# MLP up-projection with the tokens stationary, and the squared features turned by DMA transposes of 16-bit planes

## The chip, the cores and the metric

The kernel is one program on one core of a Trainium2 chip. The metric is the time of one execution on the device in microseconds (us); the value of a kernel is the median of its runs. The engines are named as in the profile: PE (TensorE, the matrix engine; PEld is its loading of stationary tiles), ACT (ScalarE), DVE (VectorE), POOL (GpSimd) and SP (SyncE), whose queue issues all DMAs of this kernel.

## The reference

Two layers over 256 tokens of width 2048, all in float32. A layer is a token mixer, a cross-attention into 256 memory tokens, and a dense MLP; each is wrapped in RMS norms and added to the residual stream. The change touches the MLP alone:

```
def squared_relu_mlp(h, w_up, w_down):          # h 256 x 2048, w_up 2048 x 8192, w_down 8192 x 2048
    return jnp.square(jax.nn.relu(h @ w_up)) @ w_down

y = squared_relu_mlp(rms_norm(h, g_mlp_pre[l]), w_up[l], w_down[l])
h = h + rms_norm(y, g_mlp_post[l])
```

## The kernel before, in words

**Split products.** Every large product is made of three matmuls. A float32 operand is split into a high part in the matmul's own type (float32r, `h` for weights, first plane of `xt` for activations) and the rest (`l`, second plane), and high x high, high x low and low x high are summed in PSUM.

**Weights.** They are streamed as units of two 128-row tiles by 512 columns (512 KB), in the order of use. For each unit `load` issues a DMA into one of 5 `r` buffers; `convert` lets ACT write the high part `h` (times the norm's gain `gT`, one instruction for each tile, where there is a gain) and then DVE the low part `l`, into one of 8 pairs of buffers. A load waits until DVE has read the unit that was 5 earlier from the same buffer; a conversion waits until PE has used the unit that was 8 earlier.

**The MLP.** The 8192 hidden features are taken in 4 groups (`q`) of 2048. In a group, 4 up panels (`p`) of 512 features are computed over 16 k-tiles (8 units), and then 4 down panels of 512 output columns over the group's 16 tiles of hidden features (8 units). The down panels go through `gemm_a`: a 128x128 tile of hidden features is stationary and 512 weight columns move, 96 matmuls to a panel, 3 for each k-tile and token block (`tb`, 128 tokens each). Since the stationary tile must have the features on its partitions, the hidden features are needed with features on partitions and tokens along the free axis.

**Up panels.** All but the first of a layer go through `gemm_w`: 128 weight columns are stationary and the tokens move, so the result has its features on the partitions already. For each k-tile and each of 4 column blocks there is one matmul of 512 columns (the weights' `h` by both planes of `xt`) and one of 256 (`l` by the high plane). Four PSUM banks come out, one for each block, each with the two halves side by side; `relu2` adds the halves, clamps, squares and splits into `h` and `lo`. The first up panel of a layer goes through `gemm_a` (tokens stationary, one token block after the other), and `relu2_t` turns its result round with four PE transposes to a token block.

**Order.** The program is written out ahead of time by one pass that keeps its own estimate of each engine's clock. `spawn` puts a side task on a heap, `run_side` continues those whose time has come, and `yield self.when(tile)` sets the task aside until the estimate says that the tile is there. Each engine then works through its own list in order, and SP its DMAs in order too. All engine calls go through a recording wrapper, so every instruction of before has line 84 in the profile, whatever function it comes from; the names of tiles tell them apart. In names, `p` is a PSUM bank, `t` a scratch tile (hidden features among them), `xt` the MLP's input, turned; PE rows give the moving operand first and the stationary one second.

Of the kernel before, what the change touches and what calls it, by code (L numbers as in the profile page):

```python
# [12 lines left out]
F32 = mybir.dt.float32  # L13
F32R = mybir.dt.float32r
I32 = mybir.dt.int32
AF = mybir.ActivationFunctionType
OP = mybir.AluOpType
AX = mybir.AxisListType
# [98 lines left out]
class Gen:  # L117
# [169 lines left out]
    def convert(self, u):  # L287
# [7 lines left out]
        if u.gains is None:  # L295
            a = slice(0, n)
            nc.scalar.activation(u.h[:, :, a], u.raw[:, :, a], AF.Copy)
            (nc.gpsimd if u.pool else nc.vector).tensor_sub(u.l[:, :, a], u.raw[:, :, a], u.h[:, :, a].bitcast(F32))
        else:
            for k in range(u.nk):  # L300
                g = self.gain_col(u.gains[k])
                nc.scalar.activation(u.h[:, k, :n], u.raw[:, k, :n], AF.Copy, scale=g)
                if u.pool:
# [127 lines left out]
    def rsqrt(self, out, v, eng=None, times=None):  # L431
# [38 lines left out]
    def square_sum(self, src, out):  # L470
        self.nc.scalar.activation(self.junk[:, :src.shape[-1]], src, AF.Square, accum_out=out)


    def setup(self):
# [28 lines left out]
        nc.sync.dma_start(self.cst[:, 128:], io["cst"][:, 128:])  # L503
        posi = c.tile([128, 4], I32, name="posi")
        nc.sync.dma_start(posi[:, 0:2], io["positions"].rearrange("o (t p) -> p (o t)", p=128))
# [9 lines left out]
        def more():  # L515
# [3 lines left out]
            nc.tensor.transpose(b[:, 128:224], graw3[0:96, :], self.ident[0:96, 0:96])  # L519
            nc.scalar.activation(self.gT[:, 32:128], b[:, 128:224], AF.Copy)  # L520
            nc.tensor.transpose(b[:, :80], graw2[0:80, :], self.ident[0:80, 0:80])
            nc.scalar.activation(self.gT[:, 128:208], b[:, :80], AF.Copy)
            yield self.T_TAB
# [913 lines left out]
    def mlp(self, l, P, last):  # L1437
        nc = self.nc
        ep, rs = self.ep, self.rs
        lhs, mov, both = self.xlhs(ep), self.xmov(), self.xboth()  # L1440
        y = [[None] * 4, [None] * 4]
        ssq = [self.st(), self.st()]

        def relu2(banks, pair):
            r = self.tt((2, 256))
            for j in range(2):
                nc.scalar.activation(r[:, j, :], banks[j][:, 256:512], AF.Copy)
            for j in range(2):
                nc.vector.tensor_add(r[:, j, :], banks[j][:, 0:256], r[:, j, :])
            nc.vector.scalar_tensor_tensor(r, r, 0.0, r, op0=OP.max, op1=OP.mult)  # L1450
            h, lo = pair
            nc.scalar.activation(h, r, AF.Copy)
            nc.vector.tensor_sub(lo, r, h.bitcast(F32))

        def relu2_t(tb, bank, pairs):
            r = self.tt()
            nc.scalar.activation(r, bank, AF.Relu)
            nc.vector.tensor_mul(r, r, r)
            yield self.when(r)
            b = self.ps()  # L1460
            for j in range(4):
                nc.tensor.transpose(b[:, j * 128:j * 128 + 128], r[:, j * 128:j * 128 + 128], self.ident)
            a = slice(tb * 128, tb * 128 + 128)
            v = b.rearrange("p (k t) -> p k t", k=4)
            for j in range(2):
                nc.scalar.activation(pairs[j][0][:, :, a], v[:, 2 * j:2 * j + 2, :], AF.Copy)
            for j in range(2):
                h, lo = pairs[j]
                nc.vector.tensor_sub(lo[:, :, a], v[:, 2 * j:2 * j + 2, :], h[:, :, a].bitcast(F32))
            self.ready.add(("up0", l, tb))  # L1470
        for q in range(4):
            hid = []
            for p in range(4):
                pairs = [(self.tt((2, 256), F32R), self.tt((2, 256), F32R)) for _ in range(2)]
                hid += pairs
                if q + p == 0:
                    for tb in range(2):
                        b = self.gemm_a(P["up", 0], lhs, (tb,))
                        self.spawn(relu2_t(tb, b[tb], pairs))
                        self.run_side()  # L1480
                else:
                    banks = self.gemm_w(P["up", 4 * q + p], 4, mov, both)
                    for j in range(2):
                        relu2(banks[2 * j:2 * j + 2], pairs[j])
            if q == 3:
                post = self.load_post("g_mlp_post", l)
                XT = None if last else self.new_xt()
                r2 = self.st()
                nc.vector.tensor_mul(r2[:, 0:2], rs[:, 0:2], rs[:, 0:2])
                nc.vector.tensor_mul(r2[:, 2:4], r2[:, 0:2], r2[:, 0:2])  # L1490
                nc.vector.tensor_scalar(r2[:, 2:4], r2[:, 2:4], 1.0 / D, None, op0=OP.mult)

            def hlhs(kt, tb):
                if q == 0:
                    self.require(("up0", l, tb))
                h, lo = hid[kt // 2]
                a = slice(tb * 128, tb * 128 + 128)
                return h[:, kt % 2, a], lo[:, kt % 2, a]

            def evac(tb, p, bank):  # L1500
                if q == 0:
                    y[tb][p] = self.tt()
                    nc.scalar.activation(y[tb][p], bank, AF.Copy)
                else:
                    nc.vector.tensor_add(y[tb][p], y[tb][p], bank)
                if q == 3:
                    self.square_sum(y[tb][p], ssq[tb][:, p:p + 1])
                    yg = self.tt()
                    nc.vector.tensor_mul(yg, y[tb][p], post[p])
                    y[tb][p] = yg  # L1510
            for p in range(4):
                if q == 3 and p == 3:
                    for tb in range(2):
                        self.part_mean(ssq[tb], r2[:, 2 + tb:3 + tb])
                    for tb in range(2):
                        b = self.gemm_a(P["dn", q, p], hlhs, (tb,))
                        evac(tb, p, b[tb])
                        self.spawn(self.chain(tb, y[tb], ssq[tb], XT, self.rs, self.ep, r2, late=8.0))
                        self.run_side()
                else:  # L1520
                    b = self.gemm_a(P["dn", q, p], hlhs)
                    for tb in range(2):
                        evac(tb, p, b[tb])

# [47 lines left out]
```

## Time and profile before

| | us |
|---|---|
| median of 3 runs (lowest to highest) | 2470.06 (2468.72 to 2470.64) |
| the profiled execution, own time | 2468.55 |
| its span, first to last instruction | 2466.7 |
| PE busy in the span | 2434.4 (99%) |
| DVE busy | 1555.5 (63%) |
| ACT busy | 1333.0 (54%) |

The profiled execution lasts 1.85 us longer than its span, and lies 1.51 us below the median. PE is busy nearly without a break. Matmuls are pipelined, so the length of one record is not what one costs; the distance between the starts of two that follow each other is. Where an instruction names itself `p<-xt,h` it is a matmul of `gemm_w`; `p<-h,xt` is the first up panel (and the mixer's projections) and `p<-h,t` a down panel, both of `gemm_a`.

### The profile page before, as it was taken

Reading aid. Unit: us, or ns where it says so; the run is one execution under the profiler, and the core shown is the slowest. Engines: PE = TensorE matmul, PEld = TensorE weight load, DVE = VectorE, ACT = ScalarE, POOL = GpSimd, SP = SyncE. Lnnn points to the kernel's source line nnn. Section 1 sums busy time; section 2 is a strip of 40 time slices with the busy share of each in tenths; the row PEclk is TensorE's granted clock in tenths of the full one; section 3 lists DMA queues with packets and bytes.
Section 4 is the critical chain, followed back from the end, with each engine's and each line's share of the span. In section 5 each row is a group of like instructions: output and inputs, shape, how many; then the busy total and the mean of one; then the engine's idle time right before and its main releaser. Section 6 shows DMA issues by size and latency. Waiting matters only on the chain.

```text
span 2466.7 us, 34746 instructions
## 1 busy us (share of the span) xinstructions
PE 2434.4 (99%) x12803; PEld 2104.2 (85%) x12803; DVE 1555.5 (63%) x2738; ACT 1333.0 (54%) x2283; POOL 154.3 (6%) x266
## 2 busy tenths in 40 slices
PE   8999999999999999999999999999999999999998
PEld 7999988888888888888878999987788888888886
DVE  6767757566546656556576577647864565665665
ACT  7665656666545445445447566546754554544542
POOL 2000002122000000000021000004300000000001
PEclk9999999999999999999999999999999999999999
DMA  7555565546666566565646464654556656666662
GB/s 255 159 169 150 152 210 177 195 156 198 200 194 187 188 194 188 188 195 172 222 145 188 127 194 122 211 166 154 179 182 199 183 193 193 184 192 195 187 206 102
DMA packets 263207, 447.36 MB, mean 181 GB/s; under 512 B 21550, under 2 KB 77566, under 8 KB 263038
## 3 DMA queue, kind: packets, MB, share of 16 engines
q1 hardware_dynamic: 263038, 445.16, 58.1%
q8 instruction: 100, 1.64, 0.3%
q14 instruction: 69, 0.57, 0.1%
HBM read 443.00 MB, written 2.10 MB: 180 GB/s over the span
## 4 chain that ended last, share of the span: by engine, by line
PE 90%; DVE 4%; ACT 2%; POOL 1%; issue 1%; DMA 1%; SPq 0%; POOLq 0%; ACTq 0%; DVEq 0%
PE p L84 90%; DVE l L84 2%; ACT h L84 1%; DVE t L84 1%; DVE s L84 1%; POOL s L84 1%; DVE xt L84 0%; DMA r<-in_w_in_dram 0%; DMA t<-in_x_dram 0%; POOL r L84 0%; SPq L84 0%; ACT junk L84 0%; ACT t L84 0%; POOL t L84 0%; POOL l L84 0%
## 5 line engine op out<-in xcount | busy, mean ns | idle before, releaser
L84 PE MATMUL p<-h,t 128*128 128x512 f32 (+3 forms) x3072 | 934.5, 382 | 0.0
L84 DVE SCALAR_TENSOR_TENSOR l<-r,gT,h 128x512 fp32r<-128x512 f32 (+3 forms) x998 | 672.6, 726 | 274.9 <-ACT h L84 272.4
L84 ACT ACTIVATE h<-r,gT 128x512 fp32r<-128x512 f32 (+3 forms) x1008 | 635.0, 688 | 287.5 <-PE p L84 156.5
L84 PE MATMUL p<-xt,h 128*128 128x512 f32 x1920 | 678.9, 399 | 0.0
L84 PEld LDWEIGHTS p<-h,t 128*128 128x128 f32 (+1 forms) x3072 | 565.0, 185 | 109.3
L84 DVE TENSOR_TENSOR l<-r,h 128x1024 fp32r<-128x1024 f32 x346 | 423.0, 1232 | 368.4 <-ACT h L84 367.1
L84 PE MATMUL p<-l,t 128*128 128x512 f32 (+3 forms) x1536 | 584.8, 381 | 0.0
L84 ACT ACTIVATE h<-r 128x1024 fp32r<-128x1024 f32 x352 | 367.9, 1057 | 378.9 <-PE p L84 360.4
L84 PE MATMUL p<-xt,l 128*128 128x256 f32 x1920 | 539.2, 281 | 0.0
L84 PE MATMUL p<-h,xt 128*128 128x384 f32 (+3 forms) x1664 | 497.3, 367 | 2.2 <-ACT h L84 2.1
L84 PEld LDWEIGHTS p<-xt,h 128*128 128x128 f32 x1920 | 360.8, 188 | 89.8
L84 PEld LDWEIGHTS p<-xt,l 128*128 128x128 f32 x1920 | 362.7, 189 | 0.3
L84 PEld LDWEIGHTS p<-h,xt 128*128 128x128 f32 x1664 | 308.8, 188 | 32.5 <-ACT h L84 2.5
L84 PEld LDWEIGHTS p<-l,t 128*128 128x128 f32 (+1 forms) x1536 | 283.6, 185 | 53.7
L84 PE MATMUL p<-l,xt 128*128 128x384 f32 (+3 forms) x832 | 299.9, 360 | 2.9 <-POOL l L84 1.4
L84 ACT ACTIVATE t<-p 128x256 f32<-128x256 f32 (+6 forms) x336 | 140.9, 445 | 124.6 <-PE p L84 123.0
L84 PEld LDWEIGHTS p<-l,xt 128*128 128x128 f32 x832 | 156.9, 189 | 17.1 <-DVE l L84 2.8
L84 POOL TENSOR_SCALAR t<-t,s 128x512 f32<-128x512 f32 x12 | 25.4, 2113 | 1752.6 <-DVE s L84 1743.7
L84 DVE TENSOR_TENSOR t<-p,t 128x256 f32<-128x256 f32 (+3 forms) x220 | 98.1, 474 | 43.5 <-ACT junk L84 18.9
L84 PE MATMUL p<-t,t 128*128 128x128 f32 (+5 forms) x624 | 110.0, 310 | 0.0
L84 PEld LDWEIGHTS p<-t,t 128*128 128x128 f32 (+3 forms) x624 | 93.7, 192 | 14.4 <-issue 1.3
L84 DVE TENSOR_TENSOR t<-t,t 128x512 fp32r<-128x512 f32 (+6 forms) x119 | 74.4, 625 | 46.7 <-ACT t L84 44.8
(77 smaller groups left out, 1136.4 us busy)
## 6 DMA issues: line engine op xcount, KB each, us to landing
r<-in_w_up_dram SPq DMA_DIRECT2D x256, 512.0 KB, 4.2
r<-in_w_down_dram SPq DMA_DIRECT2D x256, 512.0 KB, 4.3
r<-in_w_in_dram SPq DMA_DIRECT2D x96, 384.0 KB, 3.7
r<-in_w_out_dram SPq DMA_DIRECT2D x64, 512.0 KB, 4.0
r<-in_w_in_dram SPq DMA_DIRECT2D x47, 512.0 KB, 4.6
r<-in_w_xkv_dram SPq DMA_DIRECT2D x32, 512.0 KB, 4.0
r<-in_w_xq_dram SPq DMA_DIRECT2D x16, 512.0 KB, 4.2
r<-in_w_xo_dram SPq DMA_DIRECT2D x16, 512.0 KB, 4.3
```

The costliest lines, as they stand in the source:

```text
L84: r = f(*a, **k)
```

## The change

All up panels now go through `gemm_a`, tokens stationary, and their results have the tokens on the partitions. A new `relu2` turns them round for each token block: ACT applies the ReLU out of PSUM, DVE squares, DVE copies the 512 float32 values as 1024 16-bit halves into two planes (all even halves, then all odd ones), SP issues one DMA that transposes the 128x1024 tile of 16-bit numbers in 128x128 blocks, ACT puts the planes together again into float32 and copies out the high part, and DVE forms the low part. The PE transposes of the first panel go. The loads of the post-norm's gain stand after the first down panel of the last group, where they stood ahead of it.

```diff
-        lhs, mov, both = self.xlhs(ep), self.xmov(), self.xboth()
+        lhs = self.xlhs(ep)
...
-        def relu2(banks, pair):
-            r = self.tt((2, 256))
-            for j in range(2):
-                nc.scalar.activation(r[:, j, :], banks[j][:, 256:512], AF.Copy)
-            for j in range(2):
-                nc.vector.tensor_add(r[:, j, :], banks[j][:, 0:256], r[:, j, :])
-            nc.vector.scalar_tensor_tensor(r, r, 0.0, r, op0=OP.max, op1=OP.mult)
-            h, lo = pair
-            nc.scalar.activation(h, r, AF.Copy)
-            nc.vector.tensor_sub(lo, r, h.bitcast(F32))
-
-        def relu2_t(tb, bank, pairs):
+        def relu2(flag, bank, h, lo):
             r = self.tt()
             nc.scalar.activation(r, bank, AF.Relu)
             nc.vector.tensor_mul(r, r, r)
-            yield self.when(r)
-            b = self.ps()
-            for j in range(4):
-                nc.tensor.transpose(b[:, j * 128:j * 128 + 128], r[:, j * 128:j * 128 + 128], self.ident)
...
+            halves = r.bitcast(U16).rearrange("p (n e) -> p e n", e=2)
+            planes = self.tt((2, 512), U16)
+            nc.vector.tensor_copy(planes, halves)
+            yield self.when(planes)
+            turned = self.tt((8, 128), U16)
+            nc.sync.dma_start(turned, planes.rearrange("p e n -> p (e n)"), transpose=True)
+            yield self.when(turned)
+            nc.scalar.activation(halves, turned.rearrange("p (e a) b -> p e (a b)", e=2), AF.Copy)
+            v = r.rearrange("p (a b) -> p a b", b=128)
+            nc.scalar.activation(h, v, AF.Copy)
+            nc.vector.tensor_sub(lo, v, h.bitcast(F32))
+            self.ready.add(flag)
...
-                    banks = self.gemm_w(P["up", 4 * q + p], 4, mov, both)
-                    for j in range(2):
-                        relu2(banks[2 * j:2 * j + 2], pairs[j])
+                    b = self.gemm_a(P["up", 4 * q + p], lhs)
+                    for tb in range(2):
+                        self.spawn(relu2(("up", l, q, p, tb), b[tb], *hid[p][tb]))
+                    self.run_side()
...
             def hlhs(kt, tb):
-                if q == 0:
-                    self.require(("up0", l, tb))
-                h, lo = hid[kt // 2]
+                self.require(("up", l, q, kt // 4, tb))
+                h, lo = hid[kt // 4][tb]
...
                     b = self.gemm_a(P["dn", q, p], hlhs)
+                    if q == 3 and p == 0:
+                        post = self.load_post("g_mlp_post", l)
```

**PE in an up panel.** Before, one k-tile of a panel (`h1598` and `l1598` hold its weights, the four banks are p1594 to p1597) stands so on PE:

```order
L84 MATMUL p1594_9376<-xt1076_3_5538,h1598_9388 128x512
L84 MATMUL p1594_9376<-xt1076_3_5538,l1598_9389 128x256
L84 MATMUL p1595_9377<-xt1076_3_5538,h1598_9388 128x512
L84 MATMUL p1595_9377<-xt1076_3_5538,l1598_9389 128x256
L84 MATMUL p1596_9378<-xt1076_3_5538,h1598_9388 128x512
L84 MATMUL p1596_9378<-xt1076_3_5538,l1598_9389 128x256
L84 MATMUL p1597_9379<-xt1076_3_5538,h1598_9388 128x512
L84 MATMUL p1597_9379<-xt1076_3_5538,l1598_9389 128x256
```

With the change, one k-tile stands so (two banks, p1492 for the first token block and p1493 for the second):

```order
L85 MATMUL p1492_7942<-h1472_7851,xt1076_1_5536 128x512
L85 MATMUL p1492_7942<-l1472_7852,xt1076_1_5536 128x512
L85 MATMUL p1492_7942<-h1472_7851,xt1076_1_5536 128x512
L85 MATMUL p1493_7943<-h1472_7851,xt1076_1_5536 128x512
L85 MATMUL p1493_7943<-l1472_7852,xt1076_1_5536 128x512
L85 MATMUL p1493_7943<-h1472_7851,xt1076_1_5536 128x512
```

Eight matmuls of 512 and 256 columns became six of 512; the columns are 3072 both times.

**ACT at the end of a group's last up panel.** The rows begin with the conversion of unit 6 of the coming down panel. Before, the panel's banks (p1444 to p1447) are evacuated there, and what the down panels read (t1440, t1442) is written in the same place:

```order
L84 ACTIVATE h1462_8304<-r1453_8198 128x1024 [waits DMAHW5_49,PE_49,Activation_49]
L84 ACTIVATE t1464_8318<-p1444_8136 128x256 [waits PE_49]
L84 ACTIVATE t1464_8318<-p1445_8137 128x256 [waits PE_49]
L84 ACTIVATE t1440_8132<-t1464_8318 128x512 [waits DVE_49]
L84 ACTIVATE t1465_8326<-p1446_8138 128x256 [waits PE_49]
L84 ACTIVATE t1465_8326<-p1447_8139 128x256 [waits PE_49]
L84 ACTIVATE t1442_8134<-t1465_8326 128x512 [waits DVE_49]
L84 ACTIVATE h1468_8342<-r1455_8220 128x1024 [waits DMAHW6_49,Activation_49]
```

With the change, the two ReLUs (t1516, t1519) stand there, four conversions follow (units 7 to 10), and only then the copies out of the turned tiles (t1526 and t1530, which the DMA transposes write) and the high parts that the down panels read (t1488, t1490):

```order
L85 ACTIVATE h1512_8088<-r1503_7996 128x1024 [waits DMAHW3_49,PE_49]
L85 ACTIVATE t1516_8100<-p1492_7942 128x512 [waits PE_49]
L85 ACTIVATE t1519_8105<-p1493_7943 128x512 [waits PE_49]
L85 ACTIVATE h1524_8118<-r1505_8014 128x1024 [waits DMAHW4_49,DVE_49]
L85 ACTIVATE h1528_8138<-r1507_8035 128x1024 [waits DMAHW5_49,DVE_49,PE_49]
L85 ACTIVATE h1532_8158<-r1509_8056 128x1024 [waits DMAHW6_49,DVE_49,PE_49]
L85 ACTIVATE h1534_8176<-r1511_8074 128x1024 [waits DMAHW7_49,DVE_49,PE_49]
L85 ACTIVATE t1516_8100<-t1526_8130 128x2x512 [waits DMAHW2_49,DVE_49]
L85 ACTIVATE t1488_7938<-t1516_8100 128x512 [waits Activation_49]
L85 ACTIVATE h1536_8197<-r1513_8092 128x1024 [waits DMAHW0_49,PE_49]
L85 ACTIVATE t1519_8105<-t1530_8144 128x2x512 [waits DMAHW4_49,DVE_49]
L85 ACTIVATE t1490_7940<-t1519_8105 128x512 [waits Activation_49]
```

The writing of the hidden features moved behind four conversions and one DMA each.

**SP at the same place.** With the change the two transposes stand among the loads of down-projection weights, each behind a load that waits for DVE:

```order
L85 DMA r1513_8092<-in_w_down_dram 128x2x512 [waits DMAHW3_49,DMAHW0_49,DVE_49]
L85 DMA r1525_8122<-in_w_down_dram 128x2x512 [waits DMAHW4_49,DVE_49]
L85 DMA_TRANSPOSE t1526_8130<-t1517_8103 128x8x128 [waits DMAHW2_49]
L85 DMA r1529_8142<-in_w_down_dram 128x2x512 [waits DMAHW5_49,DVE_49]
L85 DMA_TRANSPOSE t1530_8144<-t1520_8108 128x8x128
L85 DMA r1533_8162<-in_w_down_dram 128x2x512 [waits DMAHW6_49,DVE_49]
```

Before, only the loads stand there. The program has 64 transposes, two to an up panel.

## Rows read from the trace of the kernel before

**Rows 1.** The page's busy times, and its chain that ended last.

```profile
PE 2434.4 (99%) x12803; PEld 2104.2 (85%) x12803; DVE 1555.5 (63%) x2738; ACT 1333.0 (54%) x2283; POOL 154.3 (6%) x266
...
PE 90%; DVE 4%; ACT 2%; POOL 1%; issue 1%; DMA 1%; SPq 0%; POOLq 0%; ACTq 0%; DVEq 0%
```

**Rows 2.** Windows: length, PE, PEld, DVE, ACT, POOL busy, PEclk, DMA share, GB/s.

```profile
741.43:831.87 90.44, 90.44 (x514) 78.48 (x512) 56.31 (x83) 48.87 (x79) 0.00 (x0) 1.00 0.60 186
831.87:918.93 87.06, 87.06 (x386) 72.08 (x385) 48.05 (x53) 37.38 (x43) 0.00 (x0) 1.00 0.63 193
...
1923.24:2013.68 90.44, 90.44 (x513) 78.47 (x512) 56.29 (x83) 48.88 (x79) 0.00 (x0) 1.00 0.61 187
2013.68:2100.75 87.07, 87.07 (x386) 72.08 (x385) 48.08 (x53) 37.37 (x43) 0.00 (x0) 1.00 0.64 193
```

**Rows 3.** PE in order of time, up panel: start us, us, what.

```profile
741.43 0.39 PE L84 MATMUL p<-xt,h 128*128 128x512 f32 x1
741.65 0.28 PE L84 MATMUL p<-xt,l 128*128 128x256 f32 x1
741.77 0.40 PE L84 MATMUL p<-xt,h 128*128 128x512 f32 x1
```

**Rows 4.** PE in order of time, first up panel of a layer.

```profile
562.53 0.61 PE L84 MATMUL p<-h,xt 128*128 128x512 f32 x2
...
563.21 0.61 PE L84 MATMUL p<-h,xt 128*128 128x512 f32 x2
```

**Rows 5.** PE in order of time, around four PE transposes.

```profile
576.74 0.60 PE L84 MATMUL p<-cst,t 128*128 128x128 f32 x4
577.09 0.48 PE L84 MATMUL p<-h,xt 128*128 128x512 f32 x1
```

**Rows 6.** ACT, groups by shape, 741.43 to 831.87: busy us, mean ns | idle before.

```profile
L84 ACT ACTIVATE h<-r 128x1024 fp32r<-128x1024 f32 x7 | 7.3, 1056 | 8.0 <-PE p L84 7.1 <-ACT h L84 1.0
...
L84 ACT ACTIVATE t<-t 128x512 fp32r<-128x512 f32 x6 | 3.8, 632 | 8.5 <-DVE t L84 8.5
L84 ACT ACTIVATE t<-p 128x512 f32<-128x512 f32 x2 | 1.2, 598 | 0.8 <-PE p L84 0.7
```

**Rows 7.** DVE, groups by shape, same stretch.

```profile
L84 DVE TENSOR_TENSOR l<-r,h 128x1024 fp32r<-128x1024 f32 x7 | 8.5, 1225 | 7.2 <-ACT h L84 7.0
L84 DVE TENSOR_TENSOR t<-p,t 128x256 f32<-128x256 f32 x14 | 5.4, 422 | 0.3
L84 DVE TENSOR_TENSOR t<-t,t 128x512 fp32r<-128x512 f32 x6 | 4.2, 693 | 4.2 <-ACT t L84 4.2
L84 DVE SCALAR_TENSOR_TENSOR t<-t 128x512 f32<-128x512 f32 x6 | 4.2, 692 | 0.2
```

**Rows 8.** DVE, one group of the whole span.

```profile
L84 DVE TENSOR_SCALAR t<-t,s 128x512 f32<-128x512 f32 x16 | 7.2, 485 | 23.1 <-POOL s L84 23.1
```

**Rows 9.** ACT in order of time, end of a group's last up panel.

```profile
826.35 1.06 ACT L84 ACTIVATE h<-r 128x1024 fp32r<-128x1024 f32 x1 [1.76 <-PE p L84]
829.17 1.06 ACT L84 ACTIVATE h<-r 128x1024 fp32r<-128x1024 f32 x1 [1.76 <-PE p L84]
```

**Rows 10.** DMA issues: tensors, engine, count, KB each, median us to landing.

```profile
r<-in_w_up_dram SPq DMA_DIRECT2D x256, 512.0 KB, 4.2
...
r<-in_w_cmp_v_dram SPq DMA_DIRECT2D x16, 256.0 KB, 3.4
...
out_dram<-t SPq DMA_DIRECT2D x8, 256.0 KB, 2.2
```

**Rows 11.** The gain loads (256 KB): issue on SP, and landing, min/median/max.

```profile
L84 SPq DMA_DIRECT2D t<-in_g_mlp_post_dram x8: 376/430/459, 1186.9 to 2370.3; - x8
...
DMA to landing us min/median/max: 5.7/6.1/7.4
```

**Rows 12.** Loads of up weights on SP (min/median/max ns), and SP's waits, 741 to 1096.

```profile
L84 SPq DMA_DIRECT2D r<-in_w_up_dram x256: 367/368/421, 539.7 to 2334.3; - x128
...
SPq L84 <- DVE l L84: 293.0, 126, 6.7
```

More of the change, by code (lines that the diff above doesn't have):

```diff
@@ L15 @@
 I32 = mybir.dt.int32
+U16 = mybir.dt.uint16
 AF = mybir.ActivationFunctionType
@@ L1458, in relu2_t @@
             nc.vector.tensor_mul(r, r, r)
-            yield self.when(r)
-            b = self.ps()
-            for j in range(4):
-                nc.tensor.transpose(b[:, j * 128:j * 128 + 128], r[:, j * 128:j * 128 + 128], self.ident)
-            a = slice(tb * 128, tb * 128 + 128)
-            v = b.rearrange("p (k t) -> p k t", k=4)
-            for j in range(2):
[L1466 to L1470, printed above, removed]
+            halves = r.bitcast(U16).rearrange("p (n e) -> p e n", e=2)
[10 more added lines that the diff above has]
+            self.ready.add(flag)
         for q in range(4):
@@ L1473, in mlp @@
             for p in range(4):
-                pairs = [(self.tt((2, 256), F32R), self.tt((2, 256), F32R)) for _ in range(2)]
-                hid += pairs
+                hid.append([[self.tt((4, 128), F32R) for _ in range(2)] for _ in range(2)])
                 if q + p == 0:
@@ L1478, in mlp @@
                         b = self.gemm_a(P["up", 0], lhs, (tb,))
-                        self.spawn(relu2_t(tb, b[tb], pairs))
+                        self.spawn(relu2(("up", l, q, p, tb), b[tb], *hid[p][tb]))
                         self.run_side()
                 else:
-                    banks = self.gemm_w(P["up", 4 * q + p], 4, mov, both)
-                    for j in range(2):
-                        relu2(banks[2 * j:2 * j + 2], pairs[j])
+                    b = self.gemm_a(P["up", 4 * q + p], lhs)
+                    for tb in range(2):
+                        self.spawn(relu2(("up", l, q, p, tb), b[tb], *hid[p][tb]))
+                    self.run_side()
             if q == 3:
-                post = self.load_post("g_mlp_post", l)
                 XT = None if last else self.new_xt()
@@ L1491, in mlp @@
                 nc.vector.tensor_scalar(r2[:, 2:4], r2[:, 2:4], 1.0 / D, None, op0=OP.mult)
+            post = None
             def hlhs(kt, tb):
-                if q == 0:
-                    self.require(("up0", l, tb))
-                h, lo = hid[kt // 2]
-                a = slice(tb * 128, tb * 128 + 128)
-                return h[:, kt % 2, a], lo[:, kt % 2, a]
+                self.require(("up", l, q, kt // 4, tb))
+                h, lo = hid[kt // 4][tb]
+                return h[:, kt % 4, :], lo[:, kt % 4, :]
             def evac(tb, p, bank):
```

## The prediction, made before the changed kernel was run

> **What bounds the kernel now.** I read the page first: PE is busy for 99% of the span, and the chain that ended last is PE for 90% of its length [rows 1]. So a stage is worth what PE spends in it, as long as PE never waits there. The windows then show the MLP: four up panels last 90.44 us, four down panels 87.06, PE is busy for all of both, at full granted clock, and the second layer repeats it to 0.01 us [rows 2]. DVE has about 38% of an up group free, ACT 46%, the DMA engines 40% [rows 2]. SP is idle most of the time: in the 355 us from 741 to 1096 it waits 293 us for DVE's low parts [rows 12]. PE's own list is therefore what counts, and anything put on the other engines is free until it makes PE wait. The reader should look for two things: what PE gets rid of, and whether the new, longer path to the hidden features reaches the down panels in time.
>
> **What PE gets rid of.** In an up panel of before, a pair of matmuls (512 and 256 columns) starts every 741.77 - 741.43 = 0.34 to 0.36 us [rows 3]; over a group of 256 pairs that is 90.44 / 256 = 0.353 us, and 22.61 us a panel of 64 pairs. The form that replaces it stands in the trace twice. The first up panel of a layer has it with the same operands: three matmuls of 512 columns in 563.21 - 562.53 = 0.68 us [rows 4]. The down panels have it 384 times in 87.06 us, 0.2267 us each [rows 2]. A panel of 96 becomes 96 x 0.2267 = 21.76 us. The columns are the same (49,152 a panel); 32 matmuls fewer is the difference, 0.85 us a panel. Thirty panels change their form (15 in each layer, the first has it already): 30 x 0.85 = 25.4 us. The PE transposes of the first panels go too: four of them hold PE from 576.74 to 577.09, 0.35 us [rows 5], and there are four such groups, 1.4 us. Together 26.8 us.
>
> Here a rule of the Trainium skill speaks against the change. The skill's page "TensorE: Matmul & The Clock Gate", section "Back-to-back issue gap", gives an isolated matmul N/2.4 + 2.5 ns at full clock. By it a panel would cost 20.8 us before and 20.7 after, and the 30 panels would give 2.5 us, not 25.4. The trace disagrees (0.353 us a pair where the rule has 0.325, 0.2267 where it has 0.216), and I go by the trace.
>
> **What the others get.** ACT in a panel: two ReLUs from PSUM (0.598), two copies of 1024 values (I take 1.056, the row of that size) and two high parts (0.632), 4.6 us [rows 6]. Even on top of the 48.87 / 4 = 12.2 us that it has now, that is 16.8 of 21.8 us. DVE: two squarings and two low parts at 0.693, and two copies of 1024 16-bit halves with a stride, which the trace does not show; between twice the 0.485 us of a 512-wide copy-like operation [rows 8] and the 1.225 us of a 1024-wide subtraction [rows 7]. I take the dear end, since the source is strided: 5.2 us, for the 4 x 0.422 + 2 x 0.692 + 2 x 0.693 = 4.5 that go [rows 7]. DVE comes to 14.1 + 0.7 = 14.8 of 21.8 us. Both costs are nothing, hidden behind PE; conversions run up to 8 units (22 us) ahead of it, so a late one costs only once that lead is gone.
>
> **The DMA transpose, which no row shows.** There are 64 of 256 KB, 16.8 MB to the 445 MB moved now; SP issues each and, in order, stands before the next load. For the time from issue to landing, L, the nearest rows are transfers of 256 KB: 2.2 us for the stores and 3.4 for loads in 512-byte pieces [rows 10], up to 7.4 for the gain loads [rows 11]. I take 4, near the loads in small pieces. SP's own time for it, S, has 0.37 us, the issue of a load, as its lower bound [rows 12]; if each of the 64 tiles of 16x128 that the built program cuts a transpose into cost one such issue it would be 23.6. I take 2, near the lower end, since the rows show one issue for 512 KB in 256 pieces.
>
> **When the hidden features are late.** In the middle of a group they have a whole panel of time. The last panel's are the test. Let E be the end of its last matmul. The down panel takes its k-tiles in order and comes to this panel's after 72 matmuls, at E + 16.2 us (first token block) and E + 16.8 (second). The path, with durations of rows 6 and 7: both ReLUs done at E + 0.6; DVE squares and copies both blocks until E + 3.7; the first transpose stands on SP behind a load that waits for the next low part, 1.2 us more, then that load's issue: out at E + 5.4. ACT meanwhile has four conversions ahead of the first copy. Each starts when PE frees a unit: every 2.83 us now, with ACT idle for 1.76 of them [rows 9], and every 12 x 0.2267 = 2.72 us then. The fourth needs the down panel's third unit, freed at E + 8.2, so ACT is free for the copy at E + 9.4. With L = 4 the first transpose landed just then; copy and high part end at E + 11.0, the next conversion at E + 12.1. The second transpose went out behind the first's S of 2 and a load, at E + 7.8, and landed at E + 11.8; its copy and high part end at E + 13.8, its low part at E + 14.5. PE asks for that at E + 17.3 (it is the third matmul), so 2.7 us are left. The first transpose may take 4.0 + 2.7 = 6.7 us before PE waits; from there each us costs 8 us, once a group. The gain is used up at L = 6.7 + 26.8 / 8 = 10 us.
>
> With L = 4 nothing is late. The gain loads are moved behind the first down panel of the last group, and land 6.1 us after issue [rows 11]; DVE's scaling by them waits about that long twice in the kernel, and its conversions behind it, under the lead of 22 us. I price that at nothing too, and at 6 us twice if the lead were gone.
>
> **Sum.** 2468.55 - 26.8 = 2441.8 us against the profiled execution; against the median, 1.5 us higher, 2443.3. I say 2442. A measurement of this kernel can tell about 0.2%, 4.9 us, from no change.
>
> **The rivals.** *Late, but not late enough to lose* (L from 7 to 10): PE waits at the 73rd matmul of the first down panel of each group. At L = 8 it is 1.3 x 8 = 10 us, and 2452. For it: landings up to 7.4 are in the rows; against it: those are broadcast loads. *Blocks in turn*, the one on the other side: a transpose moves its eight 128x128 blocks one after another, b us each, and the second transpose follows the first. It has landed at E + 5.4 + 16b, and PE, which can bear E + 14.8, waits 16b - 9.4 us in each group: nothing up to b = 0.59, the whole gain at 0.80. A store of 256 KB puts b at 2.2 / 8 = 0.28 if a transpose is no dearer; a transfer's whole landing of 2.2 for each block would make 25.8 x 8 = 206 us, 2648 [rows 10]. Half-way, at b = 1.24, it is 10.4 x 8 = 84 us, and 2525. For it: nothing in the trace says how a transpose is spread over the DMA engines; against it: every transfer of this kernel is spread, 256 KB at 2.2. The Trainium skill's page "VectorE: DVE Perf Modes", section "The three transpose paths", gives 1309 ns for one 128x128 block of 16-bit values by DMA, against 390 on TensorE; taken for each block in turn, that is an estimate of 11.5 x 8 = 92 us of waits, 2534, and no row here shows it. *SP held*: if SP stays with a transpose for S, the second lands at about E + 8 + 2S; past S = 3.4 PE waits, and at 5.1 the gain is gone. At S = 23.6 SP itself is the bound: 8 x 23.6 + 64 x 0.37 = 212 us in a group for 174 us of PE, 38 x 8 = 304 us, and 2746. *No gain on PE*: if the 256-wide matmuls were not what costs, the time stays at 2465 to 2470; rows 3 and 4, at one clock, speak against it.
>
> **How the numbers follow.** All hidden, 2437 to 2447: 0.62, which is the forecast. Late but gaining, 2447 to 2465: 0.10. Within 0.2%: 0.05, of it 0.02 for no gain on PE. Slower: 0.23, of it 0.13 for blocks in turn and 0.10 for SP held; about 0.04 of it ends below 2480, the rest lies anywhere up to the prices above. A range of 2437 to 2480 holds 0.62 + 0.10 + 0.05 + 0.04 = 0.81. The forecast's own range is 2437 to 2447: 26.8 us with 5 us either way for the waits priced at nothing and the price of a pair. Faster: 0.62 + 0.10 = 0.72; same 0.05; slower 0.23.
>
> **What would show it.** Four up panels of 87.1 us, as long as four down panels, without a gap on PE. No wait of PE for `t` at the start of the down panels; ACT's wait for the turned tile at that place under 2.7 us. Transposes landing within 6.7 us, with the loads' landing near 4.2. Wrong it would be if PE shows a wait 16 us into each group's down panels, or if SP's issues spread apart and conversions wait for `r`.

## The result, and the profile after

The changed kernel takes 2443.3 us (median of 4 runs, 2440.14 to 2445.64) where the kernel before, beside it, takes 2469.43: a ratio of 0.9888, 95% interval 0.9877 to 0.99. That is 26.1 us less by the medians and 28.4 by the spans of the profiled executions (that of the changed kernel is the fastest of its four runs). The forecast was 2442.

The page's busy times and chain answer to [rows 1]:

```profile
PE 2405.3 (99%) x11827; PEld 2054.0 (84%) x11827; DVE 1551.9 (64%) x2678; ACT 1413.7 (58%) x2283; POOL 155.9 (6%) x266
...
DMA packets 330787, 464.06 MB, mean 190 GB/s; under 512 B 89134, under 2 KB 145150, under 8 KB 330622
...
PE 92%; DVE 4%; ACT 1%; POOL 1%; issue 1%; DMA 1%; SPq 0%; POOLq 0%; ACTq 0%; DVEq 0%
```

PE is busy for 29.1 us less and still 99% of a shorter span; ACT for 81 us more, and in the MLP PE has no wait for it. The windows are those of [rows 2], four up panels and four down panels of the first layer, and the same of the second:

```profile
737.76:824.80 87.04, 87.04 (x385) 72.07 (x384) 55.22 (x75) 56.44 (x78) 0.00 (x0) 1.00 0.75 209
824.80:911.85 87.05, 87.05 (x386) 72.07 (x385) 48.44 (x52) 40.21 (x45) 0.00 (x0) 1.00 0.68 202
1905.26:1992.30 87.04, 87.04 (x386) 72.07 (x384) 55.11 (x75) 56.15 (x78) 0.00 (x0) 1.00 0.76 209
1992.30:2079.34 87.04, 87.04 (x386) 72.07 (x384) 48.44 (x52) 40.18 (x45) 0.00 (x0) 1.00 0.68 202
```

Read the first two numbers of a row: the up panels last 87.04 us, busy throughout, as the down panels always did. 3.40 us went from each group. The DMA share rose from 0.60 to 0.75 in the up panels and from 0.63 to 0.68 in the down panels, and PE shows no gap. All waits between 737 and 1086 us, two groups of the first layer, are these (SP's own queue apart):

```profile
ACT h L85 <- PE p L85: 143.7, 101, 1.7
DVE l L85 <- ACT h L85: 116.8, 100, 1.8
DVE t L85 <- ACT t L85: 22.8, 24, 2.4
ACT t L85 <- PE p L85: 6.8, 9, 1.0
ACT t L85 <- DMA t<-t: 3.0, 6, 1.2
ACT t L85 <- DVE l L85: 0.2, 1, 0.2
```

There is no row of PE. ACT waits for a turned tile six times, 1.2 us at most.

The new operations, by group (busy, mean ns, idle before), and then the transposes on SP from 700 to 1190:

```profile
L85 ACT ACTIVATE t<-t 128x1024 uint16<-128x1024 uint16 x64 | 87.5, 1367 | 20.7 <-DMA t<-t 18.8 <-DVE l L85 1.6
...
L85 DVE COPY t<-t 128x1024 uint16<-128x1024 uint16 x64 | 44.4, 694 | 2.2
```

```profile
L85 SPq DMA_TRANSPOSE t<-t x24: 1237/1512/3274, 764.2 to 1179.9; - x24
...
DMA to landing us min/median/max: 4.6/5.7/7.2
```

So L, the time to landing, was 4.6 to 7.2 us here, with a median of 5.7 (5.8 for all 64), and S, what SP spends, mostly between 1.24 and 1.9 us, at most 3.27. The place that decided is the end of a group's last up panel, here of the second group of the first layer; its last matmul ends, and so E is, at 825.0. SP in order of time:

```profile
816.74 12.50 SPq L85 DMA_DIRECT2D r<-in_w_down_dram  x5
829.29 1.24 SPq L85 DMA_TRANSPOSE t<-t  x1
830.62 0.55 SPq L85 DMA_DIRECT2D r<-in_w_down_dram  x1
831.21 1.90 SPq L85 DMA_TRANSPOSE t<-t  x1
```

ACT at the same place; a row of `t<-t` of 2.0 us is a copy of 16-bit halves and the high part behind it:

```profile
824.33 1.28 ACT L85 ACTIVATE t<-p 128x512 f32<-128x512 f32 x2 [0.98 <-PE p L85]
...
834.13 2.02 ACT L85 ACTIVATE t<-t 128x1024 uint16<-128x1024 uint16 x2
836.06 1.04 ACT L85 ACTIVATE h<-r 128x1024 fp32r<-128x1024 f32 x1
837.41 2.04 ACT L85 ACTIVATE t<-t 128x1024 uint16<-128x1024 uint16 x2 [0.30 <-DMA t<-t]
```

And the last low part on DVE:

```profile
839.48 0.69 DVE L85 TENSOR_TENSOR t<-t,t 128x512 fp32r<-128x512 f32 x1 [1.12 <-ACT t L85]
```

It ends at 840.17, E + 15.2. PE asks at 842.26, E + 17.3: 2.1 us are left, and this is why the windows show no gap.

### The profile page after: what moved, and what is told of

Its sections match the earlier page's. It is cut to its first block, busy times and chain, and to the rows that moved or that the text cites. A ratio compares the mean times of both kernels' runs of the same rounds, so it can differ in the third digit from the quotient of the medians.

```text
span 2438.3 us, 32888 instructions
## 1 busy us (share of the span) xinstructions
PE 2405.3 (99%) x11827; PEld 2054.0 (84%) x11827; DVE 1551.9 (64%) x2678; ACT 1413.7 (58%) x2283; POOL 155.9 (6%) x266
## 2 busy tenths in 40 slices
DMA packets 330787, 464.06 MB, mean 190 GB/s; under 512 B 89134, under 2 KB 145150, under 8 KB 330622
## 4 chain that ended last, share of the span: by engine, by line
PE 92%; DVE 4%; ACT 1%; POOL 1%; issue 1%; DMA 1%; SPq 0%; POOLq 0%; ACTq 0%; DVEq 0%
PE p L85 92%; DVE l L85 2%; DVE t L85 1%; DVE s L85 1%; ACT h L85 1%; POOL s L85 1%; DVE xt L85 0%; ACT junk L85 0%; POOL r L85 0%; POOL t L85 0%; ACT t L85 0%; POOL l L85 0%; DMA t<-in_x_dram 0%; DMA r<-in_w_in_dram 0%; DMA r<-in_w_xkv_dram 0%
## 5 line engine op out<-in xcount | busy, mean ns | idle before, releaser
L85 PE MATMUL p<-h,xt 128*128 128x512 f32 (+3 forms) x3584 | 1088.2, 379 | 1.7 <-ACT h L85 1.6
L85 PEld LDWEIGHTS p<-h,xt 128*128 128x128 f32 x3584 | 668.9, 188 | 106.1 <-ACT h L85 2.0
L85 PE MATMUL p<-l,xt 128*128 128x512 f32 (+3 forms) x1792 | 673.0, 376 | 2.5 <-DVE l L85 1.4
L85 PEld LDWEIGHTS p<-l,xt 128*128 128x128 f32 x1792 | 337.1, 188 | 53.9 <-DVE l L85 2.8
L85 ACT ACTIVATE t<-p 128x512 f32<-128x512 f32 (+5 forms) x268 | 132.6, 511 | 130.8 <-PE p L85 126.8
L85 ACT ACTIVATE t<-t 128x512 fp32r<-128x512 f32 (+3 forms) x138 | 132.7, 962 | 48.0 <-DVE t L85 25.3
L85 POOL TENSOR_SCALAR t<-t,s 128x512 f32<-128x512 f32 x12 | 25.4, 2113 | 1722.7 <-DVE s L85 1721.9
L85 PE MATMUL p<-cst,t 128*128 128x128 f32 (+1 forms) x533 | 84.7, 277 | 16.8 <-DVE t L85 8.7
L85 PEld LDWEIGHTS p<-cst,t 128*128 128x128 f32 (+1 forms) x533 | 65.2, 142 | 34.2 <-issue 7.5
L85 ACT ACTIVATE t<-t,s 128x128 f32<-128x128 f32 x80 | 35.8, 448 | 91.7 <-DVE s L85 91.7
L85 ACT ACTIVATE junk<-t 128x512 f32<-128x512 f32 x80 | 50.4, 630 | 61.7 <-DVE t L85 59.6
```

The source lines that it names most:

```text
L85: r = f(*a, **k)
```

## The experiments

Two questions are open after the result. Does the gain come from where the prediction put it (fewer matmuls on PE, kept by transposes that PE does not do), and how near is the turned tile to being late? Beside the experiments the kernel before took 2469.63 to 2469.96 us, and each ratio is against it.

**PE transposes in place of the DMA.** All up panels keep the tokens stationary, but PE turns the blocks round:

```diff
-            halves = r.bitcast(U16).rearrange("p (n e) -> p e n", e=2)
-            planes = self.tt((2, 512), U16)
-            nc.vector.tensor_copy(planes, halves)
-            yield self.when(planes)
-            turned = self.tt((8, 128), U16)
-            nc.sync.dma_start(turned, planes.rearrange("p e n -> p (e n)"), transpose=True)
-            yield self.when(turned)
-            nc.scalar.activation(halves, turned.rearrange("p (e a) b -> p e (a b)", e=2), AF.Copy)
-            v = r.rearrange("p (a b) -> p a b", b=128)
+            yield self.when(r)
+            b = self.ps()
+            for j in range(4):
+                nc.tensor.transpose(b[:, j * 128:j * 128 + 128], r[:, j * 128:j * 128 + 128], self.ident)
+            v = b.rearrange("p (a b) -> p a b", b=128)
```

> All up panels stay with the tokens stationary, but their squared features are turned by four PE transposes for each token block instead of a DMA transpose. My theory: the form of the matmuls gives 25.4 us, and the DMA transposes are what keeps it, since they cost PE nothing. Then 64 blocks of four transposes at 0.35 to 0.45 us of PE each come back, 22 to 29 us: 2466 to 2472 where the changed kernel has 2443, so about as long as before. Rival: the time came from something else (the evacuations, the banks), and PE transposes hide as well: 2441 to 2447.

It took 2473.12 us (2471.05 to 2475.75), 1 us above the expected range, ratio 1.0015, interval 1.0006 to 1.0025. Against the changed kernel that is 29.8 us for 64 groups of four transposes, 0.47 us each. PE in order of time shows 0.35 of it in the transposes themselves, as in [rows 5], and 0.09 in the matmul behind them, which starts 0.32 us before the next in place of 0.23:

```profile
765.07 0.60 PE L85 MATMUL p<-cst,t 128*128 128x128 f32 x4
765.42 0.48 PE L85 MATMUL p<-h,xt 128*128 128x512 f32 x1
765.74 0.40 PE L85 MATMUL p<-l,xt 128*128 128x512 f32 x1
```

So the form with tokens stationary is worth nothing by itself: PE would give back in transposes what it saves in matmuls. The transposes by DMA are what keeps the gain.

**A second transpose ahead of each.** It goes into a scratch tile that nobody reads, so SP and the DMA engines do twice the work:

```diff
+            for _ in range(1):
+                self.tc.nc.sync.dma_start(self.scr[0], planes.rearrange("p e n -> p (e n)"), transpose=True)
             turned = self.tt((8, 128), U16)
```

> Ahead of each DMA transpose stands a second one of the same planes into a scratch tile that nothing reads; one scratch tile, so the second block's extra transpose also waits until the first block's has landed. The order of everything else is unchanged. My theory of the slack: in the changed kernel the last panel's second low part is done 15.2 us after the panel's end and PE asks for it at 17.3, so 2.1 us are left; the second real transpose goes out some 4 to 5 us later here, PE waits about 2 to 3 us in each of 8 groups, 15 to 24 us in all: 2458 to 2467. Rival, the transposes are hidden deep and a delay of a few us costs nothing: 2443. Rival, the DMA engines or SP are near their limit: over 2480, with conversions waiting for loads.

It took 2461.33 us (2454.01 to 2470.95), ratio 0.9971, interval 0.9955 to 0.9987. The new gaps on PE stand 17 to 22 us into the down groups. The windows of the group with the longest of them, and of the up panels behind it:

```profile
1826.80:1920.52 93.72, 89.61 (x385) 73.14 (x384) 47.53 (x48) 45.53 (x54) 0.00 (x0) 0.96 0.71 206
1920.52:2007.56 87.04, 87.04 (x386) 72.10 (x385) 52.73 (x74) 55.18 (x77) 0.00 (x0) 1.00 0.86 219
```

From 700 us to the end the waits of PE for ACT's `t` rise from 2.0 us (once) in the changed kernel to 11.2 us (9 times, the longest 3.4):

```profile
PE p L85 <- ACT t L85: 11.2, 9, 3.4
```

Up panels stay at 87.04 with the DMA engines at 0.86; only the beginnings of down groups suffer, as the prediction's path has it. One of the nine, 2.0 us, is in the changed kernel too, and a wait of 1.8 in the first group lies ahead of 700: of the 20.5 us by the spans, 11.0 are such waits. Much of the rest is PE being slower in these groups. In the one shown it is busy for 89.61 us, 2.6 more than in the changed kernel, at a granted clock of 0.96.

**The gain loads back in their old place.**

```diff
             if q == 3:
+                post = self.load_post("g_mlp_post", l)
                 XT = None if last else self.new_xt()
...
-            post = None
...
-                    if q == 3 and p == 0:
-                        post = self.load_post("g_mlp_post", l)
```

> The loads of the post-norm's gain stand ahead of the last group's down panels again, as before the change. My theory: that place costs nothing either way, 2443 with 2 us to either side. Rival: DVE's wait for the gain, some 6 us in each layer, reaches PE in the changed kernel: 2431 to 2438 here.

2443.76 us (2443.07 to 2445.16), ratio 0.9897, interval 0.9882 to 0.9911: the move of these loads is worth nothing that can be measured, as the prediction priced it.

**512 columns as twice 256.** The changed kernel with each matmul of an up panel cut in two, tokens stationary as before; same columns, twice the matmuls:

```diff
+                    for s in range(2):
+                        c = slice(256 * s, 256 * s + 256)
+                        o = banks[tb][:, c]
+                        mm(o, xh, h[:, k, c], start=i == 0 and s == 0, stop=False, skip_group_check=True)
+                        mm(o, xh, l[:, k, c], start=False, stop=False, skip_group_check=True)
+                        mm(o, xl, h[:, k, c], start=False, stop=i == total - 1 and s == 1, skip_group_check=True)
...
-                    b = self.gemm_a(P["up", 4 * q + p], lhs)
+                    b = self.gemm_half(P["up", 4 * q + p], lhs)
```

> In the up panels each matmul of 512 columns is made of two of 256 with the same stationary tile, 192 to a panel. Three theories of what the 256-wide matmuls of before cost. A fixed price for each matmul, as the prediction has it (0.2267 us is 512 columns at 2.4 GHz and 13 ns): 192 x 0.120 = 23.0 us a panel, 32 panels, 41 us more: 2484. A 256-wide matmul is too short to hide the load of the next 128-column stationary tile, and takes 0.126 us whatever goes with it (0.353 less 0.2267): 24.2 us a panel, 80 us more: 2523. Columns alone count, and only the mixing of two widths costs: 2443.

2481.05 us (2480.28 to 2481.93), ratio 1.0048. The window of four up panels:

```profile
743.01:835.16 92.15, 92.15 (x769) 92.15 (x768) 55.34 (x75) 56.08 (x78) 0.00 (x0) 1.00 0.71 201
```

92.15 / 768 = 0.1200 us for 256 columns, against 0.2267 for 512. Doubling the columns adds 0.1067, so, if every column costs the same, a matmul costs 0.0133 us beside its columns. That is the fixed price of the prediction, and the other two expectations (nothing but columns, or the load of the stationary tile as the bound) are out; but by it a pair of before would cost 0.2267 + 0.1200 = 0.3467, and [rows 2, 3] have 0.353. Of the 0.85 us a panel, 32 x 0.0133 = 0.43 is fewer matmuls; 64 x 0.0066 = 0.42 is something else about the pair.

**Each transpose twice into the same tile.** The second has to wait for the landing of the first, which makes the turned tile late by one landing:

```diff
             nc.sync.dma_start(turned, planes.rearrange("p e n -> p (e n)"), transpose=True)
+            self.tc.nc.sync.dma_start(turned, planes.rearrange("p e n -> p (e n)"), transpose=True)
```

> The changed kernel with every transpose issued twice, the second into the same tile as the first, so that it can start only when the first has landed. It tells what a late turned tile does. By the path at the end of a group, the two blocks now need four transposes in a row on SP: the first block lands about 12 us after its issue in place of 6, and SP stands still meanwhile, so the second block's pair follows it, and its features come about 9 us after PE asks for them. PE should then wait with each group's first down panel, at the 73rd matmul, some 7 to 10 us: 8 groups make 55 to 80 us, 2500 to 2525, with waits of PE for t of just that size. In the up panels SP loses some 12 us for each pair, so loads may come late too, which would lengthen the up panels beyond 21.8 us each and add to it. Rival: the turned tiles were never near the end of the path, and the lead of 8 units absorbs SP's standing still: 2443 to 2448.

2587.62 us (one run): the place and kind of the wait were as expected, the size twice that. Each group has two waits, 14.3 to 15.6 us together. In the group whose down panels begin at 842.9, PE first waits 16 us in, in order of time:

```profile
869.03 0.79 PE L85 MATMUL p<-h,t 128*128 128x512 f32 x1 [9.65 <-ACT t L85]
875.62 0.79 PE L85 MATMUL p<-h,t 128*128 128x512 f32 x1 [4.94 <-ACT t L85]
```

ACT shows why it is 14.6 us and not 7 to 10:

```profile
842.25 2.03 ACT L85 ACTIVATE t<-t 128x1024 uint16<-128x1024 uint16 x2 [7.30 <-DMA t<-t]
...
848.81 2.03 ACT L85 ACTIVATE t<-t 128x1024 uint16<-128x1024 uint16 x2 [3.59 <-DMA t<-t]
850.75 2.94 ACT L85 ACTIVATE h<-r 128x1024 fp32r<-128x1024 f32 x3
853.59 1.06 ACT L85 ACTIVATE t<-p 128x512 f32<-128x512 f32 x2
```

ACT works in order and stands before the turned tiles of the third panel (7.30 and 3.59 us idle). The ReLUs of the fourth panel come behind them: they are done at 854.65, 11.6 us after the panel's last matmul, where the changed kernel has them done 0.6 us after it. The lateness of one panel is handed to the next. A second loss is the clock. The windows of this group are from its start to the first wait, over the waits, and to its end; then the three matmuls between the two waits, and two us shortly after the second:

```profile
842.90:859.00 16.10, 16.10 (x73) 13.32 (x71) 9.72 (x11) 11.06 (x13) 0.00 (x0) 1.00 0.79 239
859.00:885.00 26.00, 11.41 (x40) 8.42 (x39) 12.15 (x13) 10.15 (x11) 0.00 (x0) 0.67 0.73 206
885.00:947.17 62.17, 62.17 (x276) 51.48 (x275) 32.24 (x35) 26.17 (x30) 0.00 (x0) 1.00 0.65 195
...
869.03:870.68 1.65, 1.65 (x3) 0.79 (x3) 1.40 (x2) 0.90 (x1) 0.00 (x0) 0.50 0.74 154
880.00:882.00 2.00, 2.00 (x11) 1.65 (x10) 1.55 (x2) 0.41 (x1) 0.00 (x0) 1.00 0.75 240
```

The granted clock has a mean of 0.67 over the 26 us with the waits, and 1.00 on both sides; the matmuls right behind the first wait ran at 0.50, the lower level, and by 880 it was 1.00 again. The group lasts 104.27 us in place of 87.05: 14.6 are the waits, and 89.68 - 87.05 = 2.6 PE's longer busy time. The waits of the eight groups are 120.6 of the 147.5 us between the spans, and slower matmuls around them most of the rest. The rival, that the tile was never near the end of the path, is out.

A transpose that goes out when the one ahead of it has landed is itself quick, here the second of the pair on SP at 839.4:

```profile
L85 SPq DMA_TRANSPOSE t<-t x1: 1233/1233/1233, 839.4 to 839.4; - x1
...
DMA to landing us min/median/max: 2.8/2.8/2.8
```

So of the 5.8 us in the changed kernel about 3 are not the transpose by itself. What they are, no run shows.

**The other half of the 0.85 us.** Four kernels, all of the kernel before with one edit to the pair of `gemm_w`. First, the widths grouped in place of alternating:

```diff
                 for b in range(nblk):
                     c = slice(b * 128, b * 128 + 128)
                     mm(banks[b].rearrange("p (e t) -> p e t", e=2), h[:, k, c], xb, start=i == 0, stop=False,
                        skip_group_check=True)
+                for b in range(nblk):
+                    c = slice(b * 128, b * 128 + 128)
                     mm(banks[b][:, 0:256], l[:, k, c], xh, start=False, stop=i == total - 1, skip_group_check=True)
```

> The kernel before with one thing changed: in an up panel the four 512-wide matmuls of a k-tile come first and then its four 256-wide ones, in place of alternating. The same matmuls, operands and columns. Theory: of the 0.85 us that the change saved in a panel, half is 32 matmuls fewer at a fixed 0.0133 us, and half is that alternating widths cost 0.0066 us a pair (0.353 against 0.2267 + 0.1200). If that is paid at each change of width, a panel pays it 16 times in place of 64: 0.32 us a panel less, 30 panels 9.5 us, a median of about 2460, and a group of four up panels of 89.2 us in place of 90.4. Rival: a pair costs 0.353 us in any order (a price of the 256-wide matmul with its own load of 128 columns beside the 512-wide one): no change, 2469 to 2470.

2466.45 us (2463.28 to 2468.56), ratio 0.9984, interval 0.9975 to 0.9993. The window of four up panels:

```profile
742.55:832.34 89.79, 89.79 (x514) 78.47 (x512) 55.57 (x81) 47.74 (x78) 0.00 (x0) 1.00 0.61 188
```

0.65 us a group, where the theory had 1.2 and its rival nothing. A pair now takes 89.79 / 256 = 0.3507: of the 0.0066, 0.0025 went. The order has a part in it, but "so much at each change of width" is wrong, for that would have taken three quarters. Then three kernels changed only what the 512-wide matmul reads or how it is written (the kernel before beside them: 2469.96). The edits, in this order:

```diff
-                    mm(banks[b].rearrange("p (e t) -> p e t", e=2), h[:, k, c], xb, start=i == 0, stop=False,
-                       skip_group_check=True)
+                    mm(banks[b], h[:, k, c], xb.rearrange("p e t -> p (e t)"), start=i == 0, stop=False,
+                       skip_group_check=True)
...
+                    mm(banks[b], h[:, k, c], h[:, k, :], start=i == 0, stop=False,
+                       skip_group_check=True)
...
+                    mm(banks[b].rearrange("p (e t) -> p e t", e=2), xh[:, b % 2 * 128:b % 2 * 128 + 128], xb, start=i == 0,
+                       stop=False, skip_group_check=True)
```

> The kernel before, where the 512-wide matmul of an up panel names its moving tokens and its bank as one run of 512 columns in place of two of 256 (the two planes lie one behind the other, so the columns are the same). With the 512s of a k-tile put first they still took 0.2335 us from one to the next, where the 512-wide matmuls of the changed kernel take 0.2267; so it is less the change of width than the 512-wide matmul of this form itself. If the two runs of 256 columns are what makes it dearer, a pair falls from 0.353 to about 0.347, a group of four up panels from 90.4 to 88.8, and the time by 30 x 0.42 = 12.6 us to about 2457. If not, 90.4 and 2469.

> The kernel before, where the 512-wide matmul of an up panel moves the 512 weight columns of its k-tile in place of the tokens; the stationary tile is still 128 of those weight columns, and the 256-wide matmul is as it was. It leaves out the right product, and is for the time of a pair. If the dearer 512 columns lie in moving the tokens' tile, a pair takes 0.347 and a group 88.8; if in holding weights as the stationary tile, or in two widths in turn, it stays 0.353 and 90.4.

> The kernel before, where the 512-wide matmul of an up panel holds 128 tokens as its stationary tile in place of 128 weight columns, and moves the tokens as it did; the 256-wide matmul is as it was. It leaves out the right product, and is for the time of a pair. If the dearer 512 columns lie in holding weights, a pair takes 0.347 and a group 88.8; if in moving the tokens' tile, or in two widths in turn, it stays 0.353 and 90.4. If all three of this call stay at 0.353, it is the two widths in turn that costs, however the 512s are grouped.

They took 2469.91, 2471.04 and 2469.16 us (one run each). The window of a group of up panels, of the first of them:

```profile
743.25:833.69 90.44, 90.44 (x514) 78.39 (x512) 56.29 (x83) 48.86 (x79) 0.00 (x0) 1.00 0.61 186
```

of the second:

```profile
744.64:835.08 90.44, 90.44 (x514) 78.47 (x512) 56.29 (x83) 48.87 (x79) 0.00 (x0) 1.00 0.60 186
```

and of the third:

```profile
742.32:832.77 90.45, 90.45 (x514) 78.39 (x512) 56.08 (x83) 47.43 (x79) 0.00 (x0) 1.00 0.60 186
```

The pair stays at 0.353 us whichever operand of the 512-wide matmul is exchanged. Neither the tokens as moving operand nor the weights as stationary one is, by itself, what costs (both exchanged at once beside a 256-wide matmul was not run); a pair of a 512 and a 256 costs 0.0066 us more than the two do among their own kind. Why, and why grouping gives back only 0.0025 of it, stays open.

**The same step at two more places.** The changed kernel, with the projection of the memory tokens to keys (two panels) also with tokens stationary, and the normalised memory tokens turned by eight DMA transposes:

```diff
-        for b in self.gemm_b(P["xk", m], 4, mov):
-            t = self.tt((2, 256))
-            self.nc.scalar.activation(t.rearrange("p a b -> p (a b)"), b, AF.Copy)
-            K.append(t)
+        banks = self.gemm_a(P["xk", m], lhs)
...
+        def task(tb, bank):
+            r = self.tt()
+            self.nc.scalar.activation(r, bank, AF.Copy)
+            yield from self.turn(r)
...
+        for c in range(4):
+            for tb in range(2):
+                self.spawn(self.mem_turn(mt[tb][c], c, tb))
```

> The changed kernel with the same step done at two more places: the projection of the memory tokens to keys (two panels, tokens moving 256 wide in 192 matmuls each) takes the tokens as stationary, 96 matmuls of 512, and its result is turned by DMA transposes; and the normalised memory tokens are turned by eight DMA transposes in place of 32 PE transposes. By the measured prices two panels save 192 x 0.1199 - 96 x 0.2267 = 1.26 us each, and 32 PE transposes at 0.087 us 2.8 us: 5.3 us, 2438 in place of 2443. Rival: the turned keys come some 15 us later than before and the cross-attention of the first layer waits for them, or the eight transposes stand before loads on SP; then the gain is gone and the time is 2443 to 2450, with PE waits for t or for weights' conversions between 360 and 530 us.

2452.42 us (2450.81 to 2454.55), 9 more than the changed kernel and 2 above the rival's range. It was the rival in kind: PE waits, mostly in the first projection to keys, for the low part of a turned memory tile. Its waits for DVE's `t` are 18.3 us in the whole span, against 8.7 in the changed kernel. The longest:

```profile
419.68 1.22 PE L85 MATMUL p<-h,t 128*128 128x512 f32 x2 [5.73 <-DVE t L85]
```

The waits are not all of it. By the spans it is 12.4 us longer: PE stands idle for 10.7 us more, and is busy for 1.7 more where the prices had 5.3 less. The 50 us from 400, first in the changed kernel and then here:

```profile
400.00:450.00 50.00, 49.35 (x335) 45.19 (x334) 44.77 (x81) 38.45 (x73) 14.70 (x24) 1.00 0.60 190
...
400.00:450.00 50.00, 40.50 (x184) 32.23 (x184) 46.79 (x94) 45.71 (x85) 14.65 (x20) 0.93 0.74 182
```

The granted clock fell to 0.93 there. So the saving on PE, if it came, was lost again to slower matmuls.

One more kernel begins the normalising one output panel earlier:

```diff
-            if p == 2 and aside is not None:
-                self.spawn(aside(), 10.0)
+            if p == 1 and aside is not None:
+                self.spawn(aside(), 6.0)
```

> The kernel with more turns by DMA, where PE waited 5.7 us for the turned memory tokens, with the one change that the normalising of the memory tokens is begun one output panel (22 us) earlier. If that wait and its followers were the whole loss, the time is about 2438, 5 us under the changed kernel. Rival: other waits take its place (the cross-attention for the turned keys, weights' conversions behind the eight turns on ACT and DVE), and it stays at 2443 or above.

2453.22 us (2453.06 to 2456.53). That wait is gone, and others stand in its place, 3.40 us for a conversion and 6.90 for a DVE result:

```profile
400.62 0.79 PE L85 MATMUL p<-l,t 128*128 128x512 f32 x1 [3.40 <-DVE l L85]
416.98 1.12 PE L85 MATMUL p<-cst,t 128*128 128x128 f32 x4 [6.90 <-DVE t L85]
```

Between 380 and 440 us there is no lead for the detour over DVE, SP and ACT to hide in. No version of these experiments beats the changed kernel.

## Why the prediction was right

**The gain on PE, 25.4 us for 30 panels.** Right to 0.01 us a panel: a group fell by 3.40, that is 0.85 a panel, because both forms stood in the trace of before and were read as distances between starts. Its explanation, "32 matmuls fewer is the difference", was half right: 0.43 is that, 0.42 the dearer pair. The rule of the Trainium skill for an isolated matmul, in "TensorE: Matmul & The Clock Gate", section "Back-to-back issue gap", does not fit these runs either: at N = 256 it gives 0.109 us, and the halved matmuls took 0.1200. By that rule 2.5 us of the gain would have been left in the prediction (redone, the sum gives 2.4). The rival *no gain on PE* fell with it.

**The PE transposes, 1.4 us.** The term was a little short: with the matmul behind them, which the term left out, four transposes cost 0.47 us when done everywhere, so 1.9. With it the sum would have been 27.3; 26.1 and 28.4 were measured, and they lie within what runs of one kernel differ by.

**What the others get.** Two durations were off in opposite ways, and PE waited for neither: DVE's strided copy took 0.694, not 1.225, ACT's copy of halves 1.367, not 1.056. ACT rose from 48.87 to 56.44 us in a group's up panels, where the prediction's 16.8 a panel would be 67.2, since it left out what goes away; it had room in both cases.

**The path at the end of a group.** It stands up step by step, with E + as measured against predicted: copies on DVE done 2.7 (3.7), first transpose out 4.3 (5.4), second 6.2 (7.8), first copy on ACT 9.1 (9.4), last low part 15.2 (14.5); left 2.1 us (2.7). L was mis-sized, 4 where it was 5.8 in the median and 6.1 for the second transpose here, and S about right. The cheaper copy and the earlier issue made up for most of the longer landing; that the margin came out so near the forecast is luck. That nothing was late is not: by the prediction's own path a landing of 6.1 would still have left 0.6. The bound of 6.7 us on a landing was a little too strict, for 6.1 left 2.1.

**The price of lateness.** "From there each us costs 8 us" was too low. It counted a wait once in a group. The doubled transposes show that it goes through ACT's order into the next panel's ReLUs, and that PE came out of a long wait at a lower granted clock: 18.4 us for each of the eight groups, by the spans, where 7 to 10 were expected. In the changed kernel no down panel waits, but the 2.1 us are a thin margin: a second transpose ahead of each uses it up.

**Blocks in turn, and SP held.** Neither cost anything here. A pair of transposes had landed 8.0 us after the first went out (829.29 to 837.3), which by the rival's own sum of 16b puts b at 0.50 us at most, under the 0.59 from which PE would wait. The transpose that landed in 2.8 us puts it at 0.35 at most. Whether the eight blocks go one after another, no run shows. The Trainium skill's 1309 ns for a block ("VectorE: DVE Perf Modes", section "The three transpose paths"), taken eight times in a row, would be 10.5 us, an estimate that no landing here reaches. The packets under 512 bytes rose from 21,550 to 89,134, 1056 for each transpose. SP spent up to 3.4 us on a transpose of a middle panel, where a whole panel of time is left, but at the end of a group 1.24 us on the first and 1.45 to 1.90 on the second, where the prediction had PE wait from 3.4.

**The gain loads.** Nothing, as priced, by a run of its own.

## What to carry to other kernels

Where PE is the bound, price a form by the distance of starts in a stage that already has it, and look for it with the same neighbours: two widths side by side cost more than each does among its own kind. Work moved from PE to the queues is worth what it saves only as long as its whole detour fits in a lead that exists there; in the MLP it fitted with 2 us to spare, in the cross-attention it did not, and lost 9 in all. Before putting such a detour in, count what stands in order behind each of its waits, since ACT, working in order, handed lateness on to the next panel here.

## What the runs showed of the hardware that was not expected

- A matmul of 512 columns followed by one of 256 costs 0.353 us, the two among their own kind 0.2267 + 0.1200; four and four in groups cost 0.3507 a pair.
- A DMA transpose of 128x1024 16-bit numbers from SBUF to SBUF takes 1.24 to 1.9 us of SP's time for most, at most 3.4 (0.37 for a load of 512 KB), and 1056 packets. It landed 5.8 us after its issue in the median among the loads, and after 2.8 where it went out behind a transpose that had landed; the DMA share of 0.86 with twice as many made no up panel longer.
- Over two waits of PE, 9.65 and 4.94 us long, the granted clock was 0.67 in the mean (of the levels 1.2 and 2.4 GHz), and 1.00 in the stretches on both sides; the three matmuls between the waits ran at 0.50.
